# Two-layer block on one core: gates of two delta-rule heads in one product 512 wide, values turned in small steps, decay rows spread by a DMA

## The chip, the cores and the metric

One NeuronCore of a Trainium2 chip runs the whole program; the other cores are idle. The metric is the device time of one execution in microseconds, as the median of several runs. The engines are called as the profile calls them: PE is the tensor engine (its weight loads are PEld), DVE the vector engine, ACT the scalar engine, POOL GpSimd; SP only issues DMAs.

## The reference, cut to what matters

Two transformer layers over 512 tokens of width 1024, in fp32. The first is stick-breaking attention and a gated feed-forward part; the change leaves it alone, but for a few constants. The second mixes two branches: a gated delta rule with 8 heads (keys 128 wide, values 256 wide) and a retention with 4 heads, then a feed-forward part. The delta-rule branch of the second layer is what the change is about:

```python
qa, ka, va, za, beta_logit, a_dt, ..., gate_a, gate_b = split(rmsnorm(x) @ w_in)
q, k, v = silu(causal_depthwise_conv(qa, ka, va))        # q and k then l2-normed
beta = sigmoid(beta_logit)
g = -exp(a_log) * softplus(a_dt + dt_bias)               # one number per token and head
g_cum = cumsum(g)                                        # within a chunk
decay = exp(where(causal, g_cum[:, None] - g_cum[None, :], -inf))
t_inv = inverse(eye + strict_lower(beta * (k @ k.T) * decay))
# scan over chunks:
#   v_new = t_inv @ (beta * (v - exp(g_cum) * (k @ state)))
#   o     = (q * exp(g_cum)) @ state + ((q @ k.T) * decay) @ v_new
#   state = state * exp(g_last) + (k * exp(g_last - g_cum)).T @ v_new
oa = rmsnorm(o) * silu(za)                               # za: the gates of a head, 256 wide
ya = oa @ w_br_a
mix = (sigmoid(gate_a) * ya + sigmoid(gate_b) * yb) @ w_out
```

The reference cuts the sequence into chunks of 64; the kernel uses chunks of 128, so a head has four.

## The kernel before

Every large product is done in three fp32r products: both operands are split into a high and a low part, and high x high, high x low and low x high are added in PSUM (`mm3`). Weights are loaded by SP in pieces of 1 MB (`raw`, two buffers), then split by ACT (the cast to `wh`) and DVE (the difference `wl`), with four buffers each. `feat_gemm` has the weights stationary and 512 tokens moving: one unit is 24 matmuls of 512 columns, and leaves features on partitions. `tok_gemm` has the tokens stationary and the weights moving, and leaves tokens on partitions. PSUM has eight banks: four under the tag "a", two under "o", two under "g". Large tiles live in 32 slots handed out in turn; a slot that is taken again waits for its last user.

The order of the work is written by hand and then refined: `mixer2` calls the large products one after another, and small work runs beside them as generators. `beside(gen)` starts one; each `yield ns` says how many nanoseconds of PE work (counted by a formula in `mm` and `tr`) are to pass before its next step; `poll`, called between the matmuls of a product, runs the steps that are due; `drain` runs all that are left, and `until` runs them till a condition holds. The program is then ordered, engine by engine, by a planner with its own costs and due times when it is built; each engine follows its list in order, and waits on semaphores.

The stages of the delta rule, with their names:

- `first_proj` projects beta and a_dt (16 columns, loaded through a `raw` buffer) together with q and k of heads 0 and 1. `qk_proj` does q and k of one further head. Its results go through `conv`: ACT copies the PSUM bank out twice, DVE adds three taps.
- `gates_and_decays` computes g, its cumulative sums and their exponentials by token. `decay_rows` makes, for four heads, two tiles: `er` = exp(g_cum) along the free axis on all partitions, and `dc`, the decay matrix. Both come from PE: g, broadcast as the stationary operand, times the cumulative matrix; for `dc` the mask is added by a product with the identity.
- `prepare` (head after head, behind the decays): SiLU of q and k, norms by transposes on PE, the products k k' and k q', scaled by DVE; each head's matrix goes to DRAM and its 32x32 diagonal blocks come back for `solve`.
- `solve`: for four heads, 31 steps of two DVE instructions (L1195, L1198), 900 ns of PE work apart. `delta_inverse` then builds the inverse of each 128x128 chunk with products on PE; POOL multiplies by masks for it (L1225).
- `values_a` is one head's v (two units of `feat_gemm`, conv and SiLU); `gates_a` is one head's za by `tok_gemm` 256 wide, with SiLU, and then the eight transposes that turn v into tokens on partitions.
- `delta_scan` is the scan of a head over four chunks, beside other work, then the norm, the multiplication by the gates, and two sets of four transposes.
- `gate` computes tanh of a slice of gate_a or gate_b and stores it in DRAM; `branch_a(part)` multiplies four heads' outputs with w_br_a.

Of the kernel before, what the change touches and what calls it, by code (L numbers as in the profile page):

```python
# [70 lines left out]
class Net:  # L71
# [360 lines left out]
    def setup(self):  # L432
# [22 lines left out]
        self.ones = self.const("ones", [P, P])  # L455
        nc.vector.memset(self.ones, 1.0)
# [4 lines left out]
        nc.vector.tensor_scalar(tri[:, 1, :], self.ones, -1.0, None, op0=ALU.mult)  # L461
        nc.vector.tensor_copy(tri[:, 2, :], self.ones)
        self.tri, self.mones, self.pones = tri[:, 0, :], tri[:, 1, :], tri[:, 2, :]
        mb = self.const("mb", [P, 2, P], BF16)

        nc.vector.tensor_scalar(mb[:, 0, :], self.cum, -NEG, NEG, op0=ALU.mult, op1=ALU.add)
        nc.vector.tensor_scalar(mb[:, 1, :], sgn[:, 1, :], NEG, None, op0=ALU.mult)
        self.mask_c, self.mask_s = mb[:, 0, :], mb[:, 1, :]
# [476 lines left out]
    def gates_and_decays(self, acc, heads):  # L945
# [41 lines left out]
        yield 7000  # L987
# [15 lines left out]
        yield from self.decay_rows(heads)  # L1003

    def decay_rows(self, heads):

        nc, S_ = self.nc, self.S
        self.decays = -1
        for h0 in range(heads[0], heads[-1], 2):
            er, dc = self.erow[h0 // 2], self.decT[h0 // 2] = S_.get([P, 2, S]), S_.get([P, 2, S])  # L1010
            ps = []
            for i in range(2):
                p = self.ps("a")
                ps.append(p)
                for n in range(NT):
                    c = slice(n * P, (n + 1) * P)
                    self.mm(p[:, c], self.g[:, n, h0 + i:h0 + i + 1].broadcast_to([P, P]), self.cum,
                            start=(n == 0), stop=False, skip_group_check=True)
                nc.scalar.activation(er[:, i, :], p, AF.Exp)
                yield 0  # L1020
            yield 1500
            for i in range(2):
                for n in range(NT):
                    c = slice(n * P, (n + 1) * P)
                    self.mm(ps[i][:, c], self.identb, self.mask_c, start=False, stop=True, skip_group_check=True)
                for n in range(NT):
                    c = slice(n * P, (n + 1) * P)
                    self.last_exp = nc.scalar.activation(dc[:, i, c], ps[i][:, c], AF.Exp,
                                                         bias=self.ngc[:, n, h0 + i:h0 + i + 1])
            yield 800  # L1030
# [17 lines left out]
    def first_proj(self, heads):  # L1048

        w = self.a["w_in_2"][0]  # L1050
        r = self.raw(w, 0, KD, O_BE, 16)
# [47 lines left out]
    def prepare(self, h):  # L1099
# [5 lines left out]
        yield 3500  # L1105
# [7 lines left out]
        yield 1600  # L1113
# [172 lines left out]
    def delta_scan(self, h):  # L1286
# [12 lines left out]
        for n in range(NT):  # L1299
# [30 lines left out]
            if n < NT - 1:  # L1330
                st = s2
                yield 600
# [343 lines left out]
```

## Time and profile before

| | us |
|---|---|
| median of 3 runs | 2145.35 (2144.69 to 2147.83) |
| the profiled execution | 2145.01 |
| its span, first to last instruction | 2142.9 |
| PE busy in the span | 2079.4 (97%) |
| DVE busy | 1134.6 (53%) |
| ACT busy | 837.8 (39%) |
| POOL busy | 172.1 (8%) |

The span is what the trace covers; the execution's own time is 2.1 us longer. Busy time of PE counts matmuls, whose ends are modelled, so a full PE is one that always has a matmul under way. The granted clock is the share of PE's full speed: 1.00 is its upper level (2.4 GHz), 0.50 its lower one (1.2 GHz). The delta rule lies at about 740 to 1290 us. In the lines of a view, `psg<-wh,s` says that a product writes PSUM tag "g", moves `wh` and has a slot's tile stationary; L135 is the line in `mm` that issues every matmul, L139 the one in `tr`.

### The profile page before, as it was taken

The numbers are of one execution on the slowest core, as the hardware profiler recorded it, in microseconds if no ns is written. First come the engines' busy times: TensorE is split into PE (matmuls) and PEld (weight loads), VectorE is DVE, ScalarE is ACT, GpSimd is POOL, SyncE is SP. The second block draws the span as 40 slices with busy tenths as digits, with TensorE's granted clock in tenths as the row PEclk, the third lists the DMA queues.
The fourth block names the chain that finished last, engine by engine and source line by source line (L and its number), as shares of the span: only waits on it lengthen the run. The fifth ranks groups of instructions, "written<-read, shape, count | busy, mean of one in ns | idle before, by whom it ended". The sixth has DMA issues, their size and how long they took to land.

```text
span 2142.9 us, 26115 instructions
## 1 busy us (share of the span) xinstructions
PE 2079.4 (97%) x10498; PEld 1757.2 (82%) x10498; DVE 1134.6 (53%) x1771; ACT 837.8 (39%) x1368; POOL 172.1 (8%) x203
## 2 busy tenths in 40 slices
PE   6899999999999899999998999999999999999998
PEld 5788878888888788888888887888888889888887
DVE  6679778333322565655756545444535475423434
ACT  3587674223212463334522432233232334322422
POOL 2000001000000133000330000010101000000000
PEclk9999999999999999999999999999999999999999
DMA  8715445323232234211342233232222363223322
GB/s 265 211 50 158 142 129 169 117 89 118 89 127 96 103 101 150 78 51 40 125 137 69 83 125 123 84 99 87 77 101 79 139 205 109 98 98 128 98 89 79
DMA packets 172568, 241.93 MB, mean 113 GB/s; under 512 B 13936, under 2 KB 120490, under 8 KB 172448
## 3 DMA queue, kind: packets, MB, share of 16 engines
q1 hardware_dynamic: 168972, 232.65, 33.2%
q0 software_dynamic: 3232, 7.34, 1.5%
q8 instruction: 82, 1.34, 0.3%
q14 instruction: 38, 0.31, 0.0%
q10 hardware_dynamic: 244, 0.29, 0.0%
HBM read 216.59 MB, written 19.41 MB: 110 GB/s over the span
## 4 chain that ended last, share of the span: by engine, by line
PE 84%; DVE 8%; DMA 3%; ACT 2%; issue 1%; POOL 1%; SPq 0%; DVEq 0%; POOLq 0%; ACTq 0%
PE psg L135 37%; PE psa L135 36%; PE pso L135 9%; DMA cv<-ada_w 2%; DVE wl L126 1%; DVE s L1198 1%; PE psa L139 1%; DVE s L1195 1%; DMA s<-ada_w 1%; DVE s L270 1%; DVE s L429 0%; DVE s L501 0%; ACT wh L122 0%; DVE cv L1042 0%; ACT s L291 0%
## 5 line engine op out<-in xcount | busy, mean ns | idle before, releaser
L135 PE MATMUL psg<-s,wh 128*128 128x512 f32 x2368 | 753.5, 398 | 2.5 <-DVE s L1521 2.0
L126 DVE TENSOR_TENSOR wl<-raw,wh 128x1024 fp32r<-128x1024 f32 x306 | 380.9, 1247 | 490.6 <-ACT wh L122 268.8
L135 PEld LDWEIGHTS psg<-s,wh 128*128 128x128 f32 x2368 | 441.1, 189 | 90.7 <-DVE s L1521 2.9
L135 PE MATMUL psa<-wh,s 128*128 128x512 f32 x1536 | 479.1, 391 | 0.3 <-ACT s L272 0.3
L135 PE MATMUL psg<-s,wl 128*128 128x512 f32 x1184 | 464.5, 392 | 0.0
L122 ACT CAST wh<-raw 128x1024 fp32r<-128x1024 f32 x202 | 212.0, 1052 | 436.9 <-PE psg L135 173.7
L135 PEld LDWEIGHTS psa<-wh,s 128*128 128x128 f32 x1536 | 289.4, 189 | 60.3 <-ACT s L272 0.7
L135 PE MATMUL psa<-wl,s 128*128 128x512 f32 x768 | 299.5, 390 | 0.3 <-DVE wl L126 0.3
L135 PEld LDWEIGHTS psg<-s,wl 128*128 128x128 f32 x1184 | 223.2, 189 | 46.7
L135 PE MATMUL psa<-s,s 128*128 128x512 f32 (+3 forms) x760 | 177.4, 364 | 1.0 <-DMA s<-sol 0.6
L135 PEld LDWEIGHTS psa<-wl,s 128*128 128x128 f32 x768 | 144.6, 188 | 30.5 <-DVE wl L126 0.6
L125 ACT CAST wh<-raw 128x1024 fp32r<-128x1024 f32 x104 | 109.1, 1050 | 153.8 <-PE psg L135 122.4
L135 PEld LDWEIGHTS psa<-s,s 128*128 128x128 f32 x760 | 131.1, 190 | 27.4 <-ACT s L1318 2.3
L135 PE MATMUL psg<-wh,s 128*128 128x256 f32 (+1 forms) x672 | 140.9, 298 | 11.0 <-ACT cv L1039 9.2
L135 PE MATMUL pso<-s,wh 128*128 128x512 f32 x448 | 137.9, 389 | 0.0
L135 PEld LDWEIGHTS psg<-wh,s 128*128 128x128 f32 x672 | 110.2, 193 | 16.9 <-ACT cv L1039 9.6
L135 PEld LDWEIGHTS pso<-s,wh 128*128 128x128 f32 x448 | 84.1, 188 | 17.5
L135 PE MATMUL psg<-wl,s 128*128 128x256 f32 (+1 forms) x336 | 97.6, 291 | 0.0
L135 PE MATMUL pso<-s,wl 128*128 128x512 f32 x224 | 87.1, 389 | 0.0
L269 ACT CAST s<-t 128x512 fp32r<-128x512 f32 (+1 forms) x94 | 54.6, 593 | 74.1 <-DVE t L1590 40.6
L270 DVE TENSOR_TENSOR s<-t,s 128x512 fp32r<-128x512 f32 (+1 forms) x94 | 69.2, 747 | 21.3 <-ACT s L269 19.9
L135 PE MATMUL psa<-s,wh 128*128 128x256 f32 x384 | 70.9, 285 | 5.8 <-ACT wh L122 3.1
(244 smaller groups left out, 2199.9 us busy)
## 6 DMA issues: line engine op xcount, KB each, us to landing
raw<-w_in SPq DMA_DIRECT2D x56, 1024.0 KB, 5.2
raw<-ffn_w_in SPq DMA_DIRECT2D x22, 1024.0 KB, 5.1
cv<-ada_w SPq DMA_DIRECT2D x64, 256.0 KB, 4.4
raw<-w_up SPq DMA_DIRECT2D x16, 1024.0 KB, 7.7
raw<-w_down SPq DMA_DIRECT2D x16, 1024.0 KB, 5.1
raw<-sb_w_qkv SPq DMA_DIRECT2D x10, 1024.0 KB
raw<-ffn_w_out SPq DMA_DIRECT2D x10, 1024.0 KB, 6.9
s<-ada_w SPq DMA_DIRECT2D x32, 256.0 KB, 7.3
```

The lines of the kernel that those rows point to most:

```text
L122: nc.scalar.copy(h, src)
L125: nc.scalar.copy(h, src)
L126: nc.vector.tensor_sub(l, src, h.bitcast(F32))
L135: self.last_mm = self.nc.tensor.matmul(acc, lhsT, rhs, **kw)
L139: self.last_mm = self.nc.tensor.transpose(out, x, ident)
L269: nc.scalar.copy(dst_h, src)
L270: nc.vector.tensor_sub(dst_l, src, dst_h.bitcast(F32))
L1195: nc.vector.tensor_mul(share, T[:, i, 0:w_].rearrange("p (o j) -> p o j", o=1).broadcast_to([nb, n, w_]), Lb[:, i, i + 1:32].rearrange("p ...
L1198: nc.vector.tensor_add(below, below, share)
```

## The change

Gates are computed for two heads at once, 512 wide, after the values of both; values are turned by token in a generator of their own (`values_t`). The decay rows are no longer made on PE: the cumulative sums are transposed once, stored in DRAM and spread over the partitions by DMAs on SP's queue, and DVE adds the bias and the mask. The scan keeps its state in the head's q and k tile and its new values in the values' tile, and adds a chunk's `attn` product one chunk later. The small weights of `first_proj` are loaded into a tile of their own. Half of gate A stands ahead of q and k of heads 2 and 3; the middle half of gate B (`gate(O_GBT, "gbD", 1, 3)`), so far ahead of `branch_a(0)`, stands behind the last heads. Several yields are longer.

```diff
--- before.py
+++ after.py
@@ -452,20 +452,19 @@
         nc.vector.memset(self.mhalf, -0.5)
         self.phalf = self.const("phalf", [P, 32])
         nc.vector.memset(self.phalf, 0.5)
-        self.ones = self.const("ones", [P, P])
-        nc.vector.memset(self.ones, 1.0)
         self.identb = self.const("identb", [P, P], BF16)
         nc.vector.tensor_copy(self.identb, self.ident)
         tri = self.const("tri", [P, 3, P], F32R)
         nc.vector.tensor_copy(tri[:, 0, :], sgn[:, 0, :])
-        nc.vector.tensor_scalar(tri[:, 1, :], self.ones, -1.0, None, op0=ALU.mult)
-        nc.vector.tensor_copy(tri[:, 2, :], self.ones)
+        nc.vector.memset(tri[:, 1, :].bitcast(F32), -1.0)
+        nc.vector.memset(tri[:, 2, :].bitcast(F32), 1.0)
         self.tri, self.mones, self.pones = tri[:, 0, :], tri[:, 1, :], tri[:, 2, :]
-        mb = self.const("mb", [P, 2, P], BF16)
-
-        nc.vector.tensor_scalar(mb[:, 0, :], self.cum, -NEG, NEG, op0=ALU.mult, op1=ALU.add)
-        nc.vector.tensor_scalar(mb[:, 1, :], sgn[:, 1, :], NEG, None, op0=ALU.mult)
-        self.mask_c, self.mask_s = mb[:, 0, :], mb[:, 1, :]
+        self.ones = self.pones.bitcast(F32)
+
+        self.mask_s = self.const("mask_s", [P, P], BF16)
+        nc.vector.tensor_scalar(self.mask_s, sgn[:, 1, :], NEG, None, op0=ALU.mult)
+        self.mask_c = self.const("mask_c", [P, P])
+        nc.vector.tensor_scalar(self.mask_c, self.cum, -NEG, NEG, op0=ALU.mult, op1=ALU.add)
         pt = self.ps("a")
         nc.tensor.transpose(pt[:, :50], rows, self.ident[:50, :50])
         self.cols = self.const("cols", [P, 50])
@@ -984,7 +983,7 @@
         g = c3("g")
         nc.vector.scalar_tensor_tensor(g, lu, -1.0, bc(alg), op0=ALU.mult, op1=ALU.mult)
         self.g = g
-        yield 7000
+        yield 9500
         pc = self.ps("a")
         gf = g.rearrange("p n h -> p (n h)")
         self.mm(pc[:, 0:32], self.cum, gf, start=True, stop=True, skip_group_check=True)
@@ -1000,34 +999,30 @@
         nc.vector.tensor_sub(fl(kd), pc[:, 32:64], fl(gc))
         nc.scalar.activation(kd, kd, AF.Exp)
         self.beta, self.ngc, self.negc, self.egl, self.kd = beta, ngc, negc, egl, kd
-        yield from self.decay_rows(heads)
+        yield 800
+
+        pg = self.ps("a")
+        self.tr(pg[:32, :P], fl(gc), self.ident)
+        rows = self.t2()
+        nc.vector.tensor_copy(rows[:32, :P], pg[:32, :P])
+        self.gcD = self.dp.tile([NT, A_H, P], F32, name="gcD")
+        nc.sync.dma_start(self.gcD.rearrange("n h c -> (n h) c"), rows[:32, :P])
+        self.decay_rows(heads)
 
     def decay_rows(self, heads):
 
         nc, S_ = self.nc, self.S
-        self.decays = -1
         for h0 in range(heads[0], heads[-1], 2):
             er, dc = self.erow[h0 // 2], self.decT[h0 // 2] = S_.get([P, 2, S]), S_.get([P, 2, S])
-            ps = []
             for i in range(2):
-                p = self.ps("a")
-                ps.append(p)
+                nc.sync.dma_start(er[:, i, :].rearrange("p (n c) -> p n c", c=P),
+                                  self.gcD[:, h0 + i, :].rearrange("(o n) c -> o n c", o=1).broadcast_to([P, NT, P]))
                 for n in range(NT):
                     c = slice(n * P, (n + 1) * P)
-                    self.mm(p[:, c], self.g[:, n, h0 + i:h0 + i + 1].broadcast_to([P, P]), self.cum,
-                            start=(n == 0), stop=False, skip_group_check=True)
-                nc.scalar.activation(er[:, i, :], p, AF.Exp)
-                yield 0
-            yield 1500
-            for i in range(2):
-                for n in range(NT):
-                    c = slice(n * P, (n + 1) * P)
-                    self.mm(ps[i][:, c], self.identb, self.mask_c, start=False, stop=True, skip_group_check=True)
-                for n in range(NT):
-                    c = slice(n * P, (n + 1) * P)
-                    self.last_exp = nc.scalar.activation(dc[:, i, c], ps[i][:, c], AF.Exp,
-                                                         bias=self.ngc[:, n, h0 + i:h0 + i + 1])
-            yield 800
+                    nc.vector.scalar_tensor_tensor(dc[:, i, c], er[:, i, c], self.ngc[:, n, h0 + i:h0 + i + 1],
+                                                   self.mask_c, op0=ALU.add, op1=ALU.add)
+                nc.scalar.activation(er[:, i, :], er[:, i, :], AF.Exp)
+                self.last_exp = nc.scalar.activation(dc[:, i, :], dc[:, i, :], AF.Exp)
         self.decays = heads[-1]
 
     def conv(self, y, acc, f):
@@ -1047,8 +1042,9 @@
 
     def first_proj(self, heads):
 
-        w = self.a["w_in_2"][0]
-        r = self.raw(w, 0, KD, O_BE, 16)
+        nc, w = self.nc, self.a["w_in_2"][0]
+        r = self.t2([P, KD, 16])
+        nc.sync.dma_start(r, w[:, O_BE:O_BE + 16].rearrange("(k p) c -> p k c", p=P))
         hl = self.t2([P, 2, KD, 16], F32R)
         h, l = hl[:, 0], hl[:, 1]
         self.evac_pair(h, l, r)
@@ -1102,7 +1098,7 @@
         nc = self.nc
         S_ = self.S
         g0 = h // 4 * 4
-        yield 3500
+        yield 9500
         if h == g0:
             self.blk[g0] = self.dp.tile([4, P, S], F32, name=f"blk{g0}")
             self.Lb[g0] = S_.get([64, 32, 32])
@@ -1110,7 +1106,7 @@
         t = self.qk[h]
         for i in range(2):
             self.silu(t[:, i, :])
-        yield 1600
+        yield 2600
         q, kk = t[:, 0, :], t[:, 1, :]
         norms = []
         pts = []
@@ -1262,17 +1258,12 @@
         self.feat_gemm(w, O_VA + h * A_DV, A_DV, self.xT, ev_v, "g")
         self.vf[h] = vf
 
-    def gates_a(self, h):
-
-        w = self.a["w_in_2"][0]
-        nc, S_ = self.nc, self.S
-        zs = self.zs[h] = S_.get([P, NT, A_DV])
-
-        def ev_z(tt, acc):
-            nc.scalar.activation(zs[:, tt, :], acc, AF.Silu)
-        self.tok_gemm(w, O_ZA + h * A_DV, self.xT, ev_z, "g", ncols=A_DV)
+    def values_t(self, h):
+
+        nc = self.nc
+        yield 7000
         vf = self.vf.pop(h)
-        vt = self.vt[h] = S_.get([P, NT, A_DV])
+        vt = self.vt[h] = self.S.get([P, NT, A_DV])
         for half in range(2):
             pt = self.ps("a", [P, 2, A_DV])
             for n2 in range(2):
@@ -1282,11 +1273,31 @@
             for n2 in range(2):
                 n = half * 2 + n2
                 nc.vector.tensor_scalar(vt[:, n, :], pt[:, n2, :], self.irk[h][:, n:n + 1], None, op0=ALU.mult)
+            yield 0
+
+    def gates_a(self, h):
+
+        nc = self.nc
+        zs = [self.S.get([P, NT, A_DV]) for _ in range(2)]
+
+        def ev_z(tt, acc):
+            for i in range(2):
+                nc.scalar.activation(zs[i][:, tt, :], acc[:, i * A_DV:(i + 1) * A_DV], AF.Silu)
+        self.tok_gemm(self.a["w_in_2"][0], O_ZA + h * A_DV, self.xT, ev_z, "g")
+        self.zs[h], self.zs[h + 1] = zs
+
+    def a_heads(self, heads):
+
+        for h in heads:
+            self.values_a(h)
+            self.beside(self.values_t(h))
+            self.beside(self.delta_scan(h))
+        self.gates_a(heads[0])
 
     def delta_scan(self, h):
         nc = self.nc
         S_ = self.S
-        while h not in self.inverted or self.scanned < h - 1:
+        while h not in self.inverted or h not in self.vt or self.scanned < h - 1:
             yield 500
         yield 1200
         vt = self.vt.pop(h)
@@ -1294,7 +1305,6 @@
         Y = self.Y[h // 2][:, h % 2, :]
         kdec, attn = self.ka[h][:, 0, :], self.ka[h][:, 1, :]
         st = None
-        vs, ss = (S_.get([P, 4, A_DV]) for _ in range(2))
         pos = []
         for n in range(NT):
             cs = slice(n * P, (n + 1) * P)
@@ -1307,31 +1317,36 @@
                 R = vt[:, n, :]
                 nc.vector.scalar_tensor_tensor(R, pk, self.negc[:, n, h:h + 1], vt[:, n, :],
                                                op0=ALU.mult, op1=ALU.add)
-                o = po[:, n % 2, :]
-                self.mm(o, q[:, cs], st, start=(n % 2 == 0), stop=False, skip_group_check=True)
+                b = slice((n - 1) * P, n * P)
+                self.mm(pos[(n - 1) // 2][:, (n - 1) % 2, :], attn[:, b], vn, start=(n == 1), stop=True,
+                        skip_group_check=True)
+                self.mm(po[:, n % 2, :], q[:, cs], st, start=(n % 2 == 0), stop=False, skip_group_check=True)
                 yield 600
             else:
                 R = vt[:, 0, :]
             pv = self.ps("a", [P, A_DV])
             self.mm(pv, Y[:, cs], R, start=True, stop=True)
-            vn = vs[:, n, :]
+            vn = vt[:, n, :]
             nc.scalar.activation(vn, pv, AF.Copy, scale=self.brk[h][:, n:n + 1])
             yield 1000
             if n < NT - 1:
                 pu = self.ps("a", [P, A_DV])
                 self.mm(pu, kdec[:, cs], vn, start=True, stop=True)
-                s2 = ss[:, n, :]
+
+                s2 = self.qk[h][:, :, cs]
+                pu = pu.rearrange("p (i c) -> p i c", i=2)
                 if n > 0:
                     nc.vector.scalar_tensor_tensor(s2, st, self.egl[:, n, h:h + 1], pu,
                                                    op0=ALU.mult, op1=ALU.add)
                 else:
                     nc.vector.tensor_copy(s2, pu)
-            self.mm(po[:, n % 2, :], attn[:, cs], vn, start=(n == 0), stop=True, skip_group_check=True)
             if n < NT - 1:
                 st = s2
                 yield 600
+            else:
+                self.mm(po[:, n % 2, :], attn[:, cs], vn, start=False, stop=True, skip_group_check=True)
         self.scanned = h
-        S_.put(vt, vs, ss, self.qk[h], self.ka[h])
+        S_.put(vt, self.qk[h], self.ka[h])
         if h % 2 == 1:
             S_.put(self.Y[h // 2])
         so = self.small([P, NT], "sm4", 12)
@@ -1339,6 +1354,8 @@
             t = self.t2([P, 2, A_DV])
             nc.scalar.activation(t, pos[half], AF.Square)
             nc.vector.tensor_reduce(out=so[:, 2 * half:2 * half + 2], in_=t, axis=AX.X, op=ALU.add)
+        while h not in self.zs:
+            yield 500
 
         f = self.small([P, NT], "sm4", 12)
         nc.vector.tensor_mul(f, self.rq[h], self.rq[h])
@@ -1353,7 +1370,7 @@
             nc.vector.scalar_tensor_tensor(z, pos[n // 2][:, n % 2, :], f2[:, n:n + 1], z,
                                            op0=ALU.mult, op1=ALU.mult)
 
-        yield 7000
+        yield 9500
         for j in range(2):
             pt = self.ps("a")
             for n in range(NT):
@@ -1546,26 +1563,23 @@
         g0, g1 = list(range(4)), list(range(4, 8))
         self.first_proj(g0)
         self.beside(self.prepare_all(g0))
+        self.gate(O_GA, "gaD", 0, 2)
         for h in (2, 3):
             self.qk_proj(h)
-        self.gate(O_GA, "gaD", 0, 4)
+        self.gate(O_GA, "gaD", 2, 4)
         self.gate(O_GBT, "gbD", 0, 1)
-        for h in g0:
-            self.values_a(h)
-            self.gates_a(h)
-            self.beside(self.delta_scan(h))
+        self.a_heads((0, 1))
+        self.a_heads((2, 3))
         for h in g1:
             self.qk_proj(h)
             if h == 4:
-                self.beside(self.decay_rows(g1))
+                self.decay_rows(g1)
                 self.beside(self.prepare_all(g1))
-        self.gate(O_GBT, "gbD", 1, 3)
         self.until(lambda: len(self.oaT) == 8)
         self.branch_a(0)
-        for h in g1:
-            self.values_a(h)
-            self.gates_a(h)
-            self.beside(self.delta_scan(h))
+        self.a_heads((4, 5))
+        self.a_heads((6, 7))
+        self.gate(O_GBT, "gbD", 1, 3)
         self.drain()
         self.branch_a(1)
         self.retention()
```

## Rows read from the trace of the kernel before

**Rows 1.** The page: busy us of each engine, share of the span, count.
```profile
PE 2079.4 (97%) x10498; PEld 1757.2 (82%) x10498; DVE 1134.6 (53%) x1771; ACT 837.8 (39%) x1368; POOL 172.1 (8%) x203
```

**Rows 2.** Windows: length; busy (count) of PE, PEld, DVE, ACT, POOL; clock, DMA, GB/s.
```profile
842.00:880.00 38.00, 36.81 (x212) 32.28 (x211) 36.11 (x82) 12.53 (x20) 4.90 (x3) 1.00 0.39 125
...
880.00:1030.00 150.00, 148.79 (x919) 130.88 (x919) 82.96 (x145) 66.39 (x120) 9.33 (x8) 1.00 0.17 51
...
1130.00:1150.00 20.00, 11.97 (x81) 11.44 (x80) 13.44 (x32) 4.31 (x8) 0.00 (x0) 0.83 0.39 120
...
1268.00:1292.00 24.00, 22.36 (x88) 15.69 (x87) 10.06 (x22) 5.44 (x10) 1.01 (x1) 0.93 0.17 56
```

**Rows 3.** Timeline of PE, last head: start, us, instruction, count, idle before and releaser.
```profile
1286.15 1.94 PE L139 MATMUL psa<-cst,s 128*128 128x128 f32 x8 [1.11 <-DVE s L1353]
```

**Rows 4.** Waits of PE: who ended them; us in total, times, longest.
```profile
PE psg L135 <- ACT cv L1039: 9.2, 2, 8.0
...
PE psa L135 <- ACT wh L122: 3.1, 2, 2.7
```

**Rows 5.** Timeline of PE: 512-wide products, then 256-wide ones.
```profile
762.58 0.62 PE L135 MATMUL psg<-s,wh 128*128 128x512 f32 x2
...
766.66 0.62 PE L135 MATMUL psg<-s,wh 128*128 128x512 f32 x2
...
973.11 0.40 PE L135 MATMUL psg<-wh,s 128*128 128x256 f32 x2
...
975.63 0.40 PE L135 MATMUL psg<-wh,s 128*128 128x256 f32 x2
```

**Rows 6.** Timeline of PE: decay rows of heads 0 to 3, and what follows.
```profile
753.58 2.03 PE L135 MATMUL psa<-cst,g 128*128 128x128 f32 x16
...
757.83 0.71 PE L135 MATMUL psg<-s,wh 128*128 128x512 f32 x2
...
759.31 0.62 PE L135 MATMUL psa<-mb,identb 128*128 128x128 bf16 x8
759.74 0.71 PE L135 MATMUL psg<-s,wh 128*128 128x512 f32 x2
```

**Rows 7.** DMA issues: count, size of each, median us from issue to landing.
```profile
raw<-w_in SPq DMA_DIRECT2D x56, 1024.0 KB, 5.2
...
cv<-ada_w SPq DMA_DIRECT2D x64, 256.0 KB, 4.4
...
s<-sol SPq DMA_DIRECT2D x32, 16.0 KB, 2.8
```

**Rows 8.** Groups of DVE, 740 to 1290 us: busy us, mean ns, idle before.
```profile
L126 DVE TENSOR_TENSOR wl<-raw,wh 128x1024 fp32r<-128x1024 f32 x70 | 86.3, 1235 | 83.9 <-ACT wh L125 67.3 <-ACT wh L122 14.6 <-PE psg L135 1.9
L1042 DVE SCALAR_TENSOR_TENSOR cv<-cr,convc,cv 128x511 f32<-128x511 f32 (+2 forms) x48 | 36.7, 765 | 0.3
...
L1195 DVE TENSOR_TENSOR s<-s,s 64x31 f32<-64x31 f32 (+15 forms) x62 | 25.5, 411 | 1.5
...
L1163 DVE SCALAR_TENSOR_TENSOR s<-psa,r,s 128x128 f32<-128x128 f32 x32 | 11.0, 343 | 0.0
```

**Rows 9.** Timeline of ACT: splits ahead of 723 us; last decay exps.
```profile
725.32 2.95 ACT L122 CAST wh<-raw 128x1024 fp32r<-128x1024 f32 x3
...
759.75 2.18 ACT L1028 ACTIVATE s<-psa,ngc 128x128 f32<-128x128 f32 x8 [0.46 <-PE psa L135]
```

**Rows 10.** Timeline of SP's queue, 690 to 752 us.
```profile
719.19 0.38 SPq L111 DMA_DIRECT2D raw<-w_in  x1
```

**Rows 11.** Timeline of POOL, 1085 to 1135 us: mask products.
```profile
1123.46 5.75 POOL L1225 TENSOR_TENSOR s<-s,cst 128x512 f32<-128x512 f32 x4
```

**Rows 12.** Timeline of DVE, 1100 to 1150 us: two solve steps.
```profile
1121.91 1.41 DVE L1198 TENSOR_TENSOR s<-s,s 64x255 f32<-64x255 f32 x1
...
1123.35 0.41 DVE L1195 TENSOR_TENSOR s<-s,s 64x252 f32<-64x252 f32 x1
```

## The prediction

> **What bounds the kernel now.** I read the page first: TensorE is busy 97% of the span and no other engine more than 53% [rows 1]. So time leaves in two ways only: less work on TensorE, or fewer waits of TensorE. For both I went to the delta rule's stretch (about 750 to 1290 us), since all but the first load and a few constants of the change lie there. The view by windows tells where TensorE is not full: 1.2 us are missing while the triangular solve of heads 0 to 3 runs beside values and gates, 1.2 us over the next 150 us, 8.0 us at 1130 to 1150, 1.6 us at the last head's end, and in the last two the granted clock is under 1 [rows 2]. That is 12.1 us of idle time. To it come matmuls at the lower clock behind a wait: eight transposes of the last head take 1.94 us and stand behind an idle 1.11 us [rows 3]; I put this at 3 us in all (an upper bound from the clock column of both stretches is 0.17 x 20 + 0.07 x 24 = 5.1 us, part of which is the idle time itself). Old waits: about 15.1 us. The waits of TensorE say who ended them: 8.0 us is one wait for ScalarE's copy out of a PSUM bank in `conv`, and 3.1 us, ahead of this stretch, are two waits for a weight split (L122) [rows 4].
>
> **Gates 512 wide.** Six periods of three 512-wide matmuls take 766.66 - 762.58 = 4.08 us, 0.2267 each; seven periods of three 256-wide ones take 975.63 - 973.11 = 2.52 us, 0.1200 each [rows 5]. A head's gates are 4 token tiles x 8 k x 3 = 96 matmuls of 256, so 768 in all become 384 of 512: 768 x 0.1200 - 384 x 0.2267 = 92.2 - 87.1. With the unrounded 0.1196 to 0.120 this is 4.8 to 5.1 us; I take -4.8. The Trainium skill's "TensorE: Matmul & The Clock Gate", section "Back-to-back issue gap", gives a lone matmul N/2.4 + 2.5 ns; by it 256 columns cost 109 ns, 512 cost 216 ns, and the pair saves 2.5 ns, 1.0 us in all (an estimate from that page). The trace shows some 13 ns over the columns for every matmul, and not 2.5, so the measured pair stands. The bytes split and loaded stay the same; a gates product now needs two weight loads and all four split buffers, as the 512-wide products of the retention part do, and that part shows no wait among TensorE's longest.
>
> **Decay rows.** Removed from TensorE for each four heads: 16 fp32 products of g with the cumulative matrix and 16 additions of the mask. For heads 0 to 3 they stand from 753.58 to 757.83 and from 759.31 to 759.74 [rows 6], 4.25 + 0.43 = 4.7 us, twice 9.4. One transpose comes in at 0.1 us. -9.3.
> What replaces them: the transposed row goes to DRAM by one DMA on SP, and eight broadcasts of 256 KB come back on SP, four a group; VectorE adds 32 times on 128x128, ScalarE does two exps 512 wide for a head in place of one of 512 and four of 128. A small DMA lands after 2.8 us, one of 256 KB after 4.4 us [rows 7], so the rows are there some 7.2 us after they are issued, plus 16 x 0.343 = 5.5 us of VectorE for a group (bound from above by L1163, which reads PSUM [rows 8]; below by nothing, if VectorE is idle there). So the last exp, at 761.9 before [rows 9], comes 6 to 9 us later. Queued behind it are the SiLUs of head 0 and, for TensorE, that head's transposes. But `prepare` now yields 6 + 1 us more ahead of them, so I cost this at 1 us (0 if the yields cover it, 7.2 + 4.4 us if VectorE stands waiting at the additions for both groups with splits behind it). On SP the later weight loads stand behind the write's wait and the broadcasts: 2.8 us and five issues at 0.38 us [rows 10], some 5 us, once. A weight load lands in 5.2 us [rows 7], and two units of 24 matmuls, 10.9 us, pass between one load and the next; hidden. Without that cover it would be 5 us.
>
> **First projection.** The gate columns' load moves from the `raw` buffers (two) to a small tile. Before, the third load of `qk_proj` is issued only at 719.19 [rows 10], when that split has freed its buffer; its split starts at 725.32 [rows 9], and TensorE waits 3.1 us for it [rows 4]. With its own tile the load goes out early: -3.1 (0 if the small tile comes free late).
>
> **Order of work.** Half of gate A before heads 2 and 3 moves 21.8 us of products and their stores; nothing is added. It covers the longer yields of `prepare`: by the yields four heads now take about 70 us and not 40, the solve starts that much later, and scans start only when the first pair's gates are nearly done. Two heads' values (21.8 us) and one 43 us block of two heads' values and gates still lie behind each scan, so I see no wait there. `gate(O_GBT, 1, 3)`, 21.8 us, moves from ahead of `branch_a(0)` to behind the last heads. There it lies beside the last scan, whose end costs 3.3 us now (1.6 idle, 0.07 x 24 clock [rows 2]); left there: 0.5 us. In the scan the late `attn` product and the state kept in the q, k tile change order and buffers, no counts: 0. The transposes of values, issued beside the next product, are as many as before: 0.
>
> **The solve's stretches.** This is the part I can't read off. Solve steps come at 0.9 us of TensorE's time, 27.9 us for a group, and take 25 us of VectorE for a group (L1195's 25.5 us over both groups, and as much again for its twin L1198 [rows 8]). Now two heads' values follow each other under it: a unit of 5.44 us asks VectorE for a split of 1.24, three conv steps of 0.77 and 4.9 of solve, 8.4 us. Over four units VectorE falls 12 us behind. Before, it was full just so (36.1 of 38 us) and TensorE lost 1.2 us, since the solve stretched and not the splits [rows 2]. The 8.0 us loss came on top: eight mask products of GpSimd, four of which take 5.75 us, lay beside the solve of heads 4 to 7, and its VectorE steps took 1.41 in place of 0.41 [rows 11, 12], so conv, and with it the PSUM bank, came late. Bounds for a group: 0 and 12 + 8 us. The nearest row is 1.2 us; I take 3 for each group, more than the row because the values are denser. New waits: 2 x 3 + 1 (decays) + 0.5 (end) = 7.5, old 15.1: -7.6.
>
> **Sum.** -4.8 - 9.3 - 3.1 - 7.6 = -24.8 us. The profiled execution took 2145.0 us (span 2142.9 and 2.1 around it), 0.3 under the median of 2145.35. So 2120.2, or about 2120.5 as a median.
>
> **Rivals.**
> All waits go: the yields and the later solve free VectorE, and GpSimd's mask products run ahead of the solve (between 842 and 880 us GpSimd is busy for 4.9 us alone [rows 2]). 2145 - 17.2 - 15.1 = 2113.
> The waits come back at their old size or a little over, at the solve of either group: 2145 - 17.2 = 2128, up to 2138 with 10 us more. For it speaks the denser values; against it that the second solve now lies beside loads of the same kind that cost 1.2 us.
> The other side: VectorE's queue becomes the bound. It is in order, so a split for TensorE stands behind every late solve step and every addition that waits for a broadcast. Price at most 2 x (12 + 8) for the solves and 7.2 + 4.4 + 2 x 5.5 for the decays, 62 us, against 32.3 us if all else goes well: 2175 at worst, some 2155 at a likelier part of it. It decides from 36.6 us of TensorE waits behind VectorE on (32.3 + 4.3). Against it: 36 of 38 us full cost 1.2 us.
> The Trainium skill's "SBUF — State Buffer", section "SBUF: two separate sides", says that a VectorE instruction with two SBUF inputs and a GpSimd instruction take one port pair in turn, each for its whole length. By that rule the 32 new additions, which read rows and mask from SBUF, can be held up like the solve steps; the steps of 1.41 us beside mask products of 1.4 us agree.
>
> **Chances.** Forecast (2113 to 2128) 0.50, all waits gone 0.17, waits back 0.20, VectorE bound and slower 0.08, gains and new waits within 0.2% of each other 0.05. A difference of 0.2% (4.3 us) is about what can be told from none here. Faster by more: 0.87, same 0.05, slower 0.08. The range leaves out the last two cases: from 2108, the best case with the clock at its upper bound (2 us less) and the gate and decay terms 1 us larger each, to 2137, near the upper end of waits that come back.
>
> **What would show it.** Right: no 256-wide products with `wh` moving in the delta rule, 384 of 512 at 0.227; no `mb` and no g products; no wait on L122 near 723; no cold transposes ahead of `branch_a(1)`; TensorE busy for some 14 us less. Wrong: a wait at head 0's transposes behind the SiLU (decays late), a wait on `conv` or on a split under either solve longer than 4 us, scans that hold PSUM banks until the gates come, or an SP queue on which weight loads land late behind the broadcasts.

## The result, and the profile after

The changed kernel takes 2115.57 us (median of 4 runs, 2113.93 to 2117.34) against 2145.77 us for the kernel before on the same chip: a ratio of 0.9858, with an interval of 0.9841 to 0.9875. On another chip the pair gave 2116.07 against 2144.86 us, 0.987 (0.9853 to 0.9886). The prediction was 2120.5 us (2108 to 2137), faster; it holds, some 5 us too high. The profiled execution of the changed kernel took 2113.93 us, its span is 2111.9.

The busy times of its page, to set against [rows 1]:

```profile
span 2111.9 us, 25187 instructions
...
PE 2060.3 (98%) x10019; PEld 1727.4 (82%) x10019; DVE 1130.0 (54%) x1803; ACT 836.2 (40%) x1347; POOL 166.7 (8%) x203
```

TensorE is busy for 19.1 us less; the span is 31.0 us shorter. Where that lies is read from the view by windows, cut into five windows at the same four points of the program in both kernels: the end of the first layer's attention, the second layer's first norm, the end of the product for beta and a_dt, and the first product of the retention that goes to PSUM tag "o". First the kernel before (window; then its length, busy time and count of each engine; granted clock, DMA share, GB/s):

```profile
0.00:325.58 325.58, 293.19 (x1600) 247.82 (x1601) 247.26 (x425) 211.99 (x382) 24.54 (x45) 0.98 0.52 159
325.58:703.67 378.09, 375.19 (x1759) 314.22 (x1758) 148.28 (x181) 110.84 (x157) 6.09 (x10) 1.00 0.35 114
703.67:739.41 35.74, 29.91 (x212) 26.23 (x211) 20.49 (x34) 15.14 (x32) 4.12 (x8) 1.00 0.39 133
739.41:1336.58 597.17, 584.94 (x3259) 505.12 (x3257) 354.92 (x671) 234.93 (x407) 93.76 (x98) 0.99 0.31 97
1336.58:2142.91 806.33, 796.20 (x3673) 663.84 (x3671) 363.65 (x460) 264.90 (x391) 43.58 (x44) 1.00 0.31 104
```

and the changed kernel, with three windows more, the two solves and the end of the last head:

```profile
0.00:322.84 322.84, 293.41 (x1600) 248.40 (x1601) 247.07 (x424) 211.89 (x382) 24.72 (x45) 0.99 0.52 161
322.84:700.87 378.03, 375.14 (x1760) 314.27 (x1759) 148.21 (x181) 110.72 (x157) 6.09 (x10) 1.00 0.36 117
700.87:733.51 32.64, 31.04 (x213) 27.40 (x211) 20.30 (x34) 15.37 (x32) 5.04 (x8) 0.95 0.35 116
733.51:1306.03 572.52, 564.62 (x2780) 473.43 (x2778) 350.85 (x704) 233.63 (x386) 87.34 (x98) 1.00 0.33 105
1306.03:2111.86 805.83, 796.09 (x3673) 663.89 (x3671) 363.61 (x460) 264.63 (x391) 43.53 (x44) 1.00 0.31 104
...
842.00:888.00 46.00, 46.00 (x213) 38.27 (x212) 39.60 (x91) 17.70 (x28) 1.20 (x2) 1.00 0.29 90
...
1095.00:1135.00 40.00, 40.00 (x186) 33.31 (x185) 34.68 (x86) 13.85 (x24) 3.01 (x3) 1.00 0.33 110
...
1240.00:1262.00 22.00, 22.00 (x103) 18.31 (x102) 8.84 (x10) 7.89 (x10) 0.00 (x0) 1.00 0.60 203
```

Four readings. The delta rule's stretch gives 597.17 - 572.52 = 24.65 us: 20.3 of TensorE's busy time and 4.3 of idle time (12.23 before, 7.90 after). The first projection gives 3.1 us: 4.2 us of idle time less (5.83 before, 1.60 after), and 1.1 us of busy time more, at a granted clock of 0.95 where it was 1.00. The attention gives 2.7 us although its code is the same: over the twelve traces kept here its end lies anywhere from 321.9 to 326.0 us, so I put that down to the execution and not to the change. And TensorE is full under both solves and at the last head's end, where [rows 2] showed gaps.

The waits of TensorE in the delta rule's stretch (738 to 1330 us; us in total, times, longest), to set against [rows 4]:

```profile
PE psa L139 <- ACT s L1041: 4.1, 1, 4.1
PE pso L135 <- DVE s L1370: 1.9, 3, 1.0
PE psa L135 <- DVE s L1342: 1.3, 3, 0.5
PE psa L135 <- DVE s L1218: 0.4, 1, 0.4
```

The 8.0 us behind `conv` and the wait for a split near 723 us are gone. A new one of 4.1 us has come: the transposes of head 0 wait for its SiLU (L1041). Around it, SP's queue, VectorE, ScalarE and TensorE of the changed kernel, from the timeline (start, length, line, count, idle before and its releaser), and last the window at 769 to 771 us:

```profile
749.88 0.33 SPq L1009 DMA_DIRECT2D gcD<-t  x1
752.53 2.02 SPq L1018 DMA_DIRECT2D s<-gcD  x4
755.01 0.70 SPq L111 DMA_DIRECT2D raw<-w_in  x1
...
757.98 3.24 DVE L1022 SCALAR_TENSOR_TENSOR s<-s,ngc,mask_c 128x128 f32<-128x128 f32 x12 [3.00 <-DMA s<-gcD]
762.87 1.14 DVE L1022 SCALAR_TENSOR_TENSOR s<-s,ngc,mask_c 128x128 f32<-128x128 f32 x4 [1.65 <-DMA s<-gcD]
...
759.16 0.64 ACT L1024 ACTIVATE s<-s 128x512 f32<-128x512 f32 x1 [5.43 <-DVE s L1022]
...
764.58 0.61 ACT L1025 ACTIVATE s<-s 128x512 f32<-128x512 f32 x1
765.20 1.28 ACT L1041 ACT_TABLE_LOAD   x1
766.49 1.15 ACT L1041 ACTIVATE s<-s 128x512 f32<-128x512 f32 x2
...
767.17 1.36 PE L139 MATMUL psa<-cst,s 128*128 128x128 f32 x8 [4.14 <-ACT s L1041]
768.19 1.21 PE L135 MATMUL psg<-s,wh 128*128 128x512 f32 x2
...
769.00:771.00 2.00, 2.00 (x6) 1.52 (x6) 1.26 (x4) 2.00 (x4) 1.38 (x2) 0.50 0.66 250
```

Read it backwards: TensorE stands for 4.14 us, then runs for some microseconds at the lower clock (two matmuls of 512 take 1.21 us, where [rows 5] has 0.62; the granted clock at 769 to 771 us is 0.50). It stands for the SiLU; that stands behind eight exps and a table load; the last two exps stand behind four additions that begin at 762.87, when the last broadcast row is there: 10.3 us after the first broadcast was issued and 13.0 us after the write. The prediction had 7.2 us from the write. The additions themselves are quicker than its bound: 16 take 4.4 us (0.27 each, against 0.343).

### The profile page after: what moved, and what is told of

Read it like the earlier page. It is cut to its first block, busy times and chain, and to the rows that moved or that the text cites. A ratio compares the mean times of both kernels' runs of the same rounds, so it can differ in the third digit from the quotient of the medians.

```text
span 2111.9 us, 25187 instructions
## 1 busy us (share of the span) xinstructions
PE 2060.3 (98%) x10019; PEld 1727.4 (82%) x10019; DVE 1130.0 (54%) x1803; ACT 836.2 (40%) x1347; POOL 166.7 (8%) x203
## 4 chain that ended last, share of the span: by engine, by line
PE 85%; DVE 6%; DMA 4%; ACT 2%; issue 1%; POOL 1%; SPq 0%; DVEq 0%; POOLq 0%; ACTq 0%
PE psg L135 37%; PE psa L135 36%; PE pso L135 9%; DMA cv<-ada_w 2%; DVE wl L126 1%; PE psa L139 1%; DMA s<-gcD 1%; DMA s<-ada_w 1%; DVE s L500 0%; DVE s L270 0%; DVE cv L1037 0%; DVE s L1194 0%; DVE s L1191 0%; PE pso L322 0%; PE pso L1513 0%
## 5 line engine op out<-in xcount | busy, mean ns | idle before, releaser
L135 PE MATMUL psa<-s,s 128*128 128x512 f32 (+3 forms) x712 | 161.7, 360 | 0.0
L135 PEld LDWEIGHTS psa<-s,s 128*128 128x128 f32 x712 | 124.1, 190 | 20.9 <-ACT s L1330 1.0
L135 PE MATMUL psg<-wh,s 128*128 128x512 f32 (+1 forms) x416 | 132.3, 380 | 1.6 <-DVE s L270 1.5
L135 PEld LDWEIGHTS psg<-wh,s 128*128 128x128 f32 x416 | 75.1, 189 | 13.3 <-DVE s L270 2.2
L270 DVE TENSOR_TENSOR s<-t,s 128x512 fp32r<-128x512 f32 (+1 forms) x94 | 69.2, 747 | 21.3 <-ACT s L269 19.9
L135 PE MATMUL psg<-wl,s 128*128 128x512 f32 (+1 forms) x208 | 74.9, 360 | 0.0
L425 POOL TENSOR_TENSOR sm<-sm,mhalf 128x1 f32<-128x1 f32 x16 | 10.1, 631 | 806.8 <-DVE sm L423 806.8
```

The lines of the kernel that those rows point to most:

```text
L135: self.last_mm = self.nc.tensor.matmul(acc, lhsT, rhs, **kw)
L270: nc.vector.tensor_sub(dst_l, src, dst_h.bitcast(F32))
L425: nc.gpsimd.tensor_tensor(out=r, in0=m, in1=self.mhalf[:, :1], op=ALU.pow)
```

## The experiments

Every time is a median; the ratio is to the kernel before on the same chip. "Stretch" is the delta rule's window as cut above: 597.17 us before, 572.52 changed (572.91 in a second trace). It is free of what the attention does in an execution. The first load through a `raw` buffer leaves the stretch's code as it is and gives 573.39, so differences under 1 us between stretches are not read; the kernel before took 2144.86 to 2146.17 us from chip to chip, so neither are differences of that size between medians of different chips.

**The kernel before, with gate B's middle half behind the last heads.** Nothing else of the change.

```diff
-        self.gate(O_GBT, "gbD", 1, 3)
         self.branch_a(0)
...
+        self.gate(O_GBT, "gbD", 1, 3)
         self.drain()
         self.branch_a(1)
```

> The kernel before with one line moved: the middle half of gate B behind the last heads. First theory (the order of work made both large waits): the last head's end loses its 3.3 to 4.5 us, and the mask products of GpSimd, which stood waiting for slots held by that gate's stores, no longer lie on the solve, so the 8 us wait and its low clock go as well, 2131 to 2134 us. Rival (the 8 us wait is of the solve and the values alone): only the end is won, about 2141 us.

Measured: 2134.5 us (2133.38 to 2136.28), ratio 0.9947 (0.9934 to 0.9961); stretch 585.14, 12.0 us less than before. Its waits and its window:

```profile
PE psa L139 <- DVE s L1353: 1.9, 3, 1.0
PE psg L135 <- ACT cv L1039: 1.3, 1, 1.3
...
740.98:1326.12 585.14, 581.08 (x3259) 502.81 (x3257) 349.12 (x671) 234.43 (x407) 93.85 (x98) 1.00 0.32 99
```

The count of matmuls is the same (x3259). Idle time falls from 12.23 to 4.06 us, and busy time by 3.9 with no matmul fewer, which I read as lower clock given back. The 8.0 us behind `conv` are gone, and so is the gap at the last head: the three waits on L1353 that are left lie at 926, 1184 and 1203 us, not at the last head, and TensorE is full, at a granted clock of 1.00, where the two stood:

```profile
1130.00:1150.00 20.00, 20.00 (x134) 18.24 (x133) 14.75 (x32) 7.62 (x13) 3.02 (x3) 1.00 0.31 96
...
1275.00:1300.00 25.00, 25.00 (x112) 20.71 (x111) 10.90 (x14) 5.27 (x5) 0.00 (x0) 1.00 0.54 175
```

So this one move ends both. How, GpSimd's timeline tells. In the kernel before it stands for 30.65 us ahead of a memset into a slot, and the masks of [rows 11] follow on the second solve:

```profile
1113.24 0.53 POOL L1218 MEMSET s<- 128x512 f32 x1 [30.65 <-issue]
```

With gate B moved, the slot is free 18 us earlier, and three pairs of masks are done by 1105.2:

```profile
1094.92 0.53 POOL L1218 MEMSET s<- 128x512 f32 x1 [9.92 <-PE psg L135]
1095.63 3.12 POOL L1225 TENSOR_TENSOR s<-s,cst 128x512 f32<-128x512 f32 x2 [0.17 <-PE psg L135]
...
1102.16 3.06 POOL L1225 TENSOR_TENSOR s<-s,cst 128x512 f32<-128x512 f32 x2
```

Slots are handed out in turn, so a product that no longer takes any at this place gives every later user another one. Which tile held the old one the trace doesn't name. It was not the tiles of that gate's stores, as the expectation has it: these were issued at 1063.29 and 1077.62 us, one landed 3.7 us after issue, and GpSimd stood until 1113.24. The other way round, this piece back at its old place in the changed kernel, was not tried: there a scan holds PSUM banks until its pair's gates are made.

**Decay rows on TensorE again**, all else changed:

```diff
-        self.gcD = self.dp.tile([NT, A_H, P], F32, name="gcD")
-        nc.sync.dma_start(self.gcD.rearrange("n h c -> (n h) c"), rows[:32, :P])
-        self.decay_rows(heads)
+        yield from self.decay_rows(heads)
...
+                    self.mm(p[:, c], self.g[:, n, h0 + i:h0 + i + 1].broadcast_to([P, P]), self.cum,
+                            start=(n == 0), stop=False, skip_group_check=True)
```

> The changed kernel with the decay rows back on TensorE, as before the change; all else as changed. First theory (the sum by rows): 9.3 us of products come back, and the 4.1 us wait ahead of head 0's transposes goes together with some 1.5 us of matmuls at the lower clock behind it, so 2115.6 + 9.3 - 5.6 = about 2119 us. Rival (that wait is of the longer order of head 0 and not of the broadcasts): the wait stays, about 2125 us.

Measured: 2118.43 us (2117.09 to 2120.86), ratio 0.9872 (0.9859 to 0.9886). The run also puts one yield ahead of the rows back from 9500 to 7000. The wait at head 0's transposes is gone; the stretch is 574.87 us, only 2.35 more than in the changed kernel. The part that was to bring the most brings little, since its stall eats most of it.

**Gates 256 wide**, one head after the other, all else changed:

```diff
+            for i in range(2):
+                zs = self.S.get([P, NT, A_DV])
...
-        self.tok_gemm(self.a["w_in_2"][0], O_ZA + h * A_DV, self.xT, ev_z, "g")
+            self.tok_gemm(self.a["w_in_2"][0], O_ZA + (h + i) * A_DV, self.xT, ev_z, "g", ncols=A_DV)
```

> The changed kernel with the gates of each head 256 wide again, both heads after each other in the same place. First theory: 384 x 25 ns less 12 columns' worth, by the two rows 4.8 us more, 2120.4 us. Rival (the formula of a lone matmul): 1 us more, 2116.6 us. Second rival (four split buffers at once hold up the next product's splits): no slower than 2115.6 us, and the short waits beside the scans shrink.

Measured: 2124.1 us (2122.33 to 2125.71), ratio 0.9897 (0.9884 to 0.9911), 8.5 us over the changed kernel. In the profiled executions 2.3 lie in the attention; the stretch is 578.60, 6.1 us longer, with 7.4 us more of busy time and 1.3 us less idle:

```profile
735.24:1313.84 578.60, 572.01 (x3165) 495.50 (x3163) 353.12 (x704) 240.00 (x390) 89.88 (x98) 1.00 0.34 104
```

**The first load through a `raw` buffer again:**

```diff
-        r = self.t2([P, KD, 16])
-        nc.sync.dma_start(r, w[:, O_BE:O_BE + 16].rearrange("(k p) c -> p k c", p=P))
+        r = self.raw(w, 0, KD, O_BE, 16)
```

> The changed kernel with the 16 gate columns loaded through a raw buffer again. First theory: the wait for the split of the third load comes back, 3.1 us more, 2118.7 us. Rival (the split would have been late anyway, or another order hides it): 2115.6 us.

Measured: 2119.79 us (2119.22 to 2120.57), ratio 0.9878 (0.9864 to 0.9891), 4.2 us over the changed kernel. The wait is back, and the first projection's window goes from 32.64 to 37.82 us, with 3.7 us more idle and 1.5 us more busy at a granted clock of 0.91, while the stretch behind it is as in the changed kernel (573.39):

```profile
PE psa L135 <- ACT wh L122: 2.6, 1, 2.6
...
701.52:739.34 37.82, 32.54 (x212) 28.79 (x211) 20.49 (x34) 15.13 (x32) 4.12 (x8) 0.91 0.37 126
```

**Head 0's transposes later**, to cover the late rows:

```diff
-        yield 2600
+        yield 8600 if h == 0 else 2600
```

> The changed kernel with one yield longer: head 0's transposes come 6 us of TensorE's work later (8600 in place of 2600), the other heads as they were. First theory (the transposes were ordered ahead of the time at which the broadcast rows, the exps and the SiLU are done): the 4.1 us wait and the low clock behind it go, 2115.6 - 5.6 = 2110 us. Rival (the time is paid later, as the solve and the scans of heads 0 to 3 start 6 us later): 2114 to 2116 us.

Measured: 2117.31 us (2115.49 to 2122.33), ratio 0.9875 (0.9861 to 0.9888); stretch 575.04. My theory fell. The wait has not gone, it is 4.95 us at another product:

```profile
769.00 0.63 ACT L1024 ACTIVATE s<-s 128x512 f32<-128x512 f32 x1 [1.56 <-DVE s L1022]
...
772.50 1.06 ACT L1397 ACTIVATE s<-psg 128x512 f32<-128x512 f32 x2
...
773.13 1.22 PE L135 MATMUL psg<-s,wh 128*128 128x512 f32 x2 [4.95 <-ACT s L1397]
```

TensorE now has other products to do, but they go to the two banks of tag "g", and the tanh of gate A (L1397) that empties these banks stands in ScalarE's queue behind the exps, the table load and the SiLU. What stalls is ScalarE's queue; the other products that TensorE got did not help, since they needed the banks that this queue empties.

**Rows stored so that each is read in one piece of 2 KB**, not four of 512 B:

```diff
+        gh = self.const("gh", [P, A_H, NT])
+        nc.vector.tensor_copy(gh, gc.rearrange("p n h -> p h n"))
...
-        self.gcD = self.dp.tile([NT, A_H, P], F32, name="gcD")
+        self.gcD = self.dp.tile([A_H, NT, P], F32, name="gcD")
...
+                nc.sync.dma_start(er[:, i, :],
+                                  self.gcD[h0 + i].rearrange("(o n) c -> o (n c)", o=1).broadcast_to([P, S]))
```

> The changed kernel with the decay rows stored in DRAM head by head, so that a broadcast reads 2 KB in one piece for each partition in place of four pieces of 512 bytes; one small copy on VectorE reorders the sums ahead of the transpose. First theory (the small pieces make the broadcasts slow: the last of four is there 10.3 us after the first is issued): they land in 5 to 7 us, the wait at head 0's transposes falls from 4.1 to under 1.5 us, 2111 to 2112 us. Rival (the time is that of the write to DRAM and of fixed parts, or of the weight load beside them): no change, 2115.6 us.

Measured: 2111.9 us (2108.16 to 2113.27), ratio 0.9847 (0.9834 to 0.986); stretch 566.34.

```profile
752.24 0.33 SPq L1011 DMA_DIRECT2D gcD<-t  x1
753.69 1.76 SPq L1020 DMA_DIRECT2D s<-gcD  x4
...
756.97 4.47 DVE L1024 SCALAR_TENSOR_TENSOR s<-s,ngc,mask_c 128x128 f32<-128x128 f32 x16 [1.48 <-DMA s<-gcD]
...
758.14 0.60 ACT L1399 ACTIVATE s<-psg 128x512 f32<-128x512 f32 x1 [3.91 <-PE psg L135]
```

All 16 additions run without a break from 3.3 us after the first broadcast's issue; the last of the four broadcasts lands 5.2 us after its issue, against 8.8 in the changed kernel. TensorE has no wait there at all. One thing goes with it: in this kernel's order a tanh (L1399) stands ahead of the exps, which in the changed kernel comes behind them. So the run shows what the edit does with the order that comes of it, not the piece size alone. The landing itself differs in a second place too: of the broadcasts for heads 4 to 7, issued two at a time, the one whose landing the trace has takes 3.4 us against 4.9. How much of the gain is the earlier landing and how much the tanh's place no run tells apart.

**Both of these.** The same two diffs together.

> The changed kernel with both the longer yield of head 0 and the rows read in pieces of 2 KB. First theory: the wait can go only once, so as the first of the two alone, 2110 us. Rival (each takes off a part): below both alone by over 2 us.

Measured: 2110.9 us (2109.16 to 2111.79), ratio 0.984 (0.9827 to 0.9853); stretch 566.51, as with the rows alone. The longer yield adds nothing.

**GpSimd products beside the solve**, in the changed kernel; eight more for each group, into a tile that nobody reads:

```diff
+            if 8 <= i < 16:
+                row = T[:, i, :].rearrange("p (o j) -> p o j", o=1).broadcast_to([nb, 16, 32])
+                nc.gpsimd.tensor_mul(extra.t.rearrange("p (o j) -> p o j", j=32), row, row)
```

> The changed kernel with eight products added on GpSimd beside steps 8 to 15 of each solve, 512 elements on 64 partitions, whose result nobody reads. First theory (a GpSimd product with two SBUF inputs stops the VectorE steps beside it, and VectorE has no room there): solve steps of 1.3 to 1.4 in place of 0.4 us, TensorE waits 4 to 8 us for each solve, 2124 to 2131 us. Rival (the solve stretches into its spare time and the splits keep theirs): the steps are slowed as well, but TensorE loses under 2 us, 2116 to 2118 us. Third possibility: no step is slowed, since the products of 64 partitions do not meet them, 2115.6 us.

Measured: 2129.1 us (2127.42 to 2131.64), ratio 0.9929 (0.9916 to 0.9941); stretch 586.36, 13.8 us longer. Waits, then rows of GpSimd and VectorE under the second solve:

```profile
PE psg L135 <- DVE wl L126: 6.8, 2, 3.7
...
PE psa L139 <- ACT cv L1041: 3.1, 2, 1.7
...
1124.07 1.41 POOL L1198 TENSOR_TENSOR s<-s 64x512 f32<-64x512 f32 x1 [1.39 <-DVE s L1195]
1126.34 1.20 POOL L1198 TENSOR_TENSOR s<-s 64x512 f32<-64x512 f32 x1 [0.86 <-DVE s L1195]
...
1124.51 1.24 DVE L1192 TENSOR_TENSOR s<-s,s 64x247 f32<-64x247 f32 x1
1125.78 0.41 DVE L1195 TENSOR_TENSOR s<-s,s 64x247 f32<-64x247 f32 x1
```

The same two steps in the changed kernel:

```profile
1112.30 0.40 DVE L1191 TENSOR_TENSOR s<-s,s 64x247 f32<-64x247 f32 x1
1112.74 0.41 DVE L1194 TENSOR_TENSOR s<-s,s 64x247 f32<-64x247 f32 x1
```

A step beside a GpSimd product takes 1.24 us where it takes 0.40 alone, much as in [rows 12]. That is the rule of the Trainium skill's "SBUF — State Buffer", section "SBUF: two separate sides" (one of the two has the shared ports for its whole instruction); these rows agree with it. Sixteen such products turn two solves that cost nothing into 9.9 us of waits for splits and for `conv`. They did not do it quite alone: the tile for the result takes a slot more, and, whether for that or not, a pair of masks (L1225 here) that in the changed kernel starts at 1130.85 us, when the second solve is done, starts at 1130.70 beside a solve that runs to 1147. What that pair costs by itself is not known.

**The changed kernel and the 2 KB rows again, side by side on one chip:**

> The changed kernel as it is, beside the next one on the same chip, so that the two can be set against each other in the same rounds. Theory (the stall behind head 0's late decay rows costs some 4 us, and reading each row in pieces of 2 KB takes it away): the changed kernel 2115 to 2117 us, the next one 2111 to 2113, 3 to 5 us apart. Rival (the stretch of the delta rule of one look was luck): both 2112 to 2117, less than 1.5 us apart.

> The changed kernel with the decay rows stored so that each is read in one piece of 2 KB, again, beside the changed kernel itself. Theory: 2111 to 2113 us, 3 to 5 us below the changed kernel of the same rounds, the stretch of the delta rule near 566 us against 572. Rival: within 1.5 us of it.

Measured: 2116.07 us (2114.57 to 2117.8) against 2109.41 us (2105.78 to 2112.43), ratios 0.987 (0.9853 to 0.9886) and 0.9836 (0.9821 to 0.985): 6.7 us apart, more than the theory's 3 to 5. The stretches are 572.91 and 566.16 us, and agree with the first traces. Idle time and lower clock both go (granted clock at 765 to 776 us: 0.84 in both traces of the changed kernel, 1.00 in both of this one):

```profile
735.76:1301.92 566.16, 562.70 (x2781) 472.24 (x2778) 350.96 (x705) 233.47 (x386) 87.72 (x98) 1.00 0.33 106
```

Against 572.52 us of the changed kernel that is 4.4 us less idle and 1.9 us less busy time. This version is the fastest of the three.

## Why the prediction was right, and where its terms were off

The direction and the mechanisms held: less work on TensorE and fewer of its waits. TensorE is busy for 19.1 us less where some 14 were forecast; gate B alone gave back 3.9 of busy time, which the forecast had among the waits. The terms of its sum, for the profiled executions:

| term | predicted, us | shown, us |
|---|---|---|
| gates 512 wide | -4.8 | -6.1 (stretch, gates 256 wide again) |
| decay rows off TensorE | -9.3 | -8.7 (574.87 on TensorE, 566.16 with 2 KB rows) |
| decay rows late | +1 | +6.4 (572.52 - 566.16) |
| first projection | -3.1 | -3.1; -5.2 by undoing it (37.82 - 32.64) |
| order: wait behind `conv`, last head's end with its clock | -12.1 (8.0 + 1.6 + 3 - 0.5) | -12.0 (gate B moved alone) |
| solves, new waits | +6 | 0 |
| gaps at 842 to 1030 us | -2.4 | -0.2 (at 880 to 1030 2.23 us are left) |

That the sum came so near is in part luck: the two largest errors, 5.4 us too little for the late rows and 6 too much for the solves, cancel. The terms shown come to -23.7 us, about the forecast's -24.8; the other 7 us of the 31.0 are the attention's 2.7 and what no run isolates.

**Gates.** Right: the stretch is longer by 5.2 to 6.1 us, by which of the three traces with the changed kernel's stretch (572.52, 572.91, 573.39) one sets against it, and 4.8 to 5.1 were worked out. The lone-matmul formula of the Trainium skill's "TensorE: Matmul & The Clock Gate", section "Back-to-back issue gap", gave 1.0 us for the pair; the run with 256 columns does not bear it out, and the rows' price of 0.1200 a matmul is nearer.

**Decay rows.** The work that leaves TensorE was sized well. The step that failed is "I cost this at 1 us": it took the landing from a row of 256 KB loads (4.4 us [rows 7]), but of four broadcasts behind each other, in pieces of 512 B, the last landed 8.8 us after its issue. And it looked for cover at one place only, the transposes' yield. The run with 8600 shows that more such cover did not help here: each engine follows its list in order, and on ScalarE's a copy out of PSUM stood behind the exps, so TensorE's other products waited too (4.95 us). The 6.4 us lie inside the bounds given (0 to 7.2 + 4.4 us), near their middle; the prediction took the low end. They hold the new place of a tanh too, so they are the price of the edit, not of the landing alone.

**First projection.** Right: the wait is gone, and the run that undoes it brings most of it back (2.6 us of 3.1). That the size agrees to a tenth is luck, since the 3.1 us are 4.2 us less idle and 1.1 us more busy at a lower granted clock, and the sum had neither the shorter wait for the split of the normed input (L270, 1.9 us before, 0.8 after) nor the clock.

**Order of work.** The sum was right, the reason in part. The prediction let the move of gate B's half end only the gap at the last head, and let the 8.0 us go with the old layout of the solve; the run with that move alone shows that it ends both. GpSimd's masks on the second solve had been read rightly [rows 11, 12], but not what had put them there.

**Solves.** The term that was mis-sized most: 3 us each, while TensorE loses nothing there. VectorE is indeed densely used (39.60 of 46 and 34.68 of 40 us), and TensorE is full all the same. GpSimd has two and three instructions in these windows; its masks lie ahead of the solves and behind them. That VectorE's density costs nothing here, while GpSimd products beside the same steps come to 13.8 us (one pair of masks among them), is what the run with extra products tells apart.

**The rivals.** "All waits go" named 2113 us; its time came within 2.6 us of the median, and its reason (masks ahead of the solve) is what the trace shows, but a new wait came that it did not have. VectorE did not become the bound. The signs given as wrong came in two places: the wait at head 0's transposes, and, small, scans that hold PSUM banks: 1.9 us in three waits, of at most 1.0, for the banks of tag "o", which the multiplication by the gates empties (L1370). The 1.3 us on L1342 are not of that kind: there the scan waits for its own first state.

**What stays open.** In the stretch the four measured parts come to -6.1 - 8.7 + 6.4 - 12.0 = -20.4 us of the 24.65. The other 4 us no run isolates; the scan's new order and buffers and the longer yields of `prepare` were not run alone. The parts were each measured in one surrounding only, so they need not add up. And the attention's 2.7 us belong to no edit.

## What to carry to other kernels

When work moves from the bounding engine to a DMA and other engines, ask which in-order queue then holds an instruction that waits for the DMA, and what stands behind it there: here a PSUM copy behind a late exp stalled TensorE though it had other products to do. Price a burst of DMAs by the last one that lands, not by the median of one. Before a wait is priced anew, ask which transfer or buffer put its parts at that place; here one moved product ended it.

## What was not expected of the hardware

Of four broadcasts of 256 KB from DRAM over 128 partitions, issued one behind the other in pieces of 512 B, the last landed 8.8 us after its issue (8.9 in the second trace), and 5.2 us in pieces of 2 KB with the same bytes (5.3 in the second). For the later broadcasts, two at a time, the landings are 4.9 and 5.2 us against 3.4 and 3.3.

The busy time that the 256-wide gates add is 7.4 us, where 0.1200 us for 768 matmuls and 0.2267 for 384 give 5.1. Ends of matmuls are modelled, and the stretch grows by 5.2 to 6.1 us, so a price beyond the start-to-start times is not shown.
